# Silu gates by one hyperbolic tangent read from PSUM, and reciprocal roots by a power on POOL, in the last two layers of a four-layer kernel

## The chip, the cores and the metric

The kernel runs on one core of a Trainium2 chip. The metric is device time in microseconds (us) of one execution; lower is better. The engines are called as in the profile: PE (TensorE, matrix products; PEld is its loading of weights), DVE (VectorE), ACT (ScalarE), POOL (GpSimd) and SP (SyncE, which only starts transfers here).

## The reference

Four layers run over 512 tokens of width 1024 in float32. The first two (attention over selected keys with a short convolution, then attention with a compressed latent, each with a feed-forward part) are not touched. The last two, with 256 context tokens beside the 512, are called layer 2 and layer 3 here, as in the kernel. Both project to q, k, v and z of width 2048, normalize q and k by head, attend, and gate the result with silu(z) ahead of an output product:

```python
def project(u, n):                      # layers 2 and 3
    q, k, v, z = jnp.split(u @ w_in, 4, axis=-1)
    q = rms_norm(q.reshape(bsz, n, HEADS, 64), qn_g)
    k = rms_norm(k.reshape(bsz, n, HEADS, 64), kn_g)
...
# layer 2: differential attention, 16 pairs of heads, values of width 128
w = p[:, :, 0] - lam * p[:, :, 1]
o = rms_norm(o, subln_g) * (1.0 - lam_init)
return (o.reshape(bsz, n, D_INNER) * jax.nn.silu(z)) @ w_out
# layer 3: neighbourhood attention, 32 heads, a band of keys and the context
out_l = (o_l * jax.nn.silu(z_l)) @ w_out
```

with `rms_norm(x, g) = x * rsqrt(mean(x*x) + EPS) * g` and `silu(z) = z * sigmoid(z)`.

## The kernel before, in words

**Products.** Every float32 product is made of three matmuls: both operands are split into a high part in fp32r and a rest. `mm3` (L587 to L589) issues high by high, low by high and high by low. The weights are split on chip: ACT casts the high part (`w_hi`, L276), POOL subtracts it (`w_lo`, L280). So each 256 columns of q, k, v or z are 24 matmuls of 256 columns on PE.

**Staging.** `second(L, nx)` runs layer L of the last two. It projects the q and k pieces of the first of 8 groups of heads, with nothing else to do beside them, and then runs a loop, `diff_run` (layer 2, 12 steps per group) or `na_run` (layer 3, 16 steps per group). A step takes one unit of 128 queries through a pipeline written out by hand: `A` scores on PE (`s`, L2105 and L2106 in layer 2, L2277 and L2278 in layer 3), `B` the row minimum of the negated scores on DVE, `E` the exponential on ACT, `Dm` the division by the row sums on DVE (L2138 to L2140, L2296 and L2297), `T` transposes on PE (L2152, L2304) whose result ACT and DVE copy out of PSUM, and `G` the product with the values. In layer 2, `Hn` and `H2` then normalize 6 blocks by head and multiply by the gate (L2193, L2194).

**What fills the steps.** The dictionaries `fill`, `extra` and `early` hold, by step number, what else is issued there: `fill` the projection pieces of the next group's q, k and v and of this group's z, `extra` and `early` small things. A matmul piece is one of the 24-matmul blocks, and its second function takes the result out of PSUM. `defer` puts a function off to the next step. Each engine takes its instructions in the order in which they are issued here, so an instruction that waits holds everything behind it on its engine.

**Gates.** A z piece (`z_piece`, 256 columns, 80 of them) is copied by ACT from PSUM to `SZ`. `gates_at` later takes `SZ` in chunks of 128 columns: ACT makes exp(-z) into `ge`, a step later DVE adds 1 (L1829) and takes the reciprocal (L1830), and POOL multiplies `SZ` by it (L1831). In layer 2 there are 12 chunks per group, in layer 3 8; the last of layer 3 falls into step 1 of the next group.

**Reciprocal roots.** `finish` makes those of q and k when all their sums of squares (`ssq`, `ssk`, 16 or 24 per partition) are there: DVE prepares, ACT takes Ln and Exp, DVE does one step of Newton's method (`rstd_parts`, L422 to L434), and then POOL multiplies the raw k or q tiles (`st`, L1800). In layer 2, q's roots are not multiplied in but go into `B` as a scale. `stack` transposes the result (L1843), ACT and DVE write it as `KH`, `KL`, `QS` (high and low parts), and `dup` has POOL issue two transfers that copy `KH` and `KL` to the other 64 partitions (L1867), for which `A` of the next group waits.

**PSUM.** During the loops the buffers called `mm`, which take projection pieces and `G`, are 2 in layer 2 and 3 in layer 3.

Of the kernel before, what the change touches and what calls it, by code (L numbers as in the profile page):

```python
# [12 lines left out]
F32 = mybir.dt.float32  # L13
# [12 lines left out]
EPS = 1e-6  # L26
NEG = -1e30
TAKEN = -3e38
UNIT = 1104
LNEXP = "natural_log_exp_and_others"  # L30


# [348 lines left out]
class Net:  # L381
# [54 lines left out]
    def rstd(s, r, ss, inv_n):  # L436
        for _ in s.rstd_parts(r, ss, inv_n):
            pass

    def run(s):  # L440
        nc, tc, io = s.nc, s.tc, s.io
        with ExitStack() as top:
# [22 lines left out]
            s.zero = s.const.tile([128, 1], F32, name="zero")  # L465
            nc.vector.memset(s.zero, 0.0)
            s.dram = s.pool("dram", 1, space=DRAM)
            s.xd = [s.dram.tile([4, 128, D], F32, name=f"xs{l}") for l in range(3)]
# [1167 lines left out]
    def tables2(s, pool, tmp):  # L1636
# [11 lines left out]
        def compute():  # L1648
# [20 lines left out]
            gs = pool.tile([128, 1], F32, name="gs")  # L1669
            nc.vector.tensor_scalar(gs, s.p("subln"), 1.0 - lam_init, None, OP.mult)  # L1670
            t2["nlam"], t2["gs"] = nlam, gs
# [3 lines left out]
    def second(s, L, nx):  # L1675
# [108 lines left out]
        def finish(n, g, k):  # L1784
            r = g2.tile([128, 24], F32, name=f"r{n}")
            rs = s.rstd_parts(r[:, :k], SS[n][:, :k], 1.0 / 64)
            next(rs)

            def two():
                next(rs, None)  # L1790
                if n == "q":
                    nc.vector.tensor_scalar(r[:, :k], r[:, :k], 0.125, None, OP.mult)
                    if diff:
                        r2 = g2.tile([128, 24], F32, name="nrq")
                        nc.vector.tensor_scalar(r2, r, -1.0, None, OP.mult)
                        scal[g] = r, r2
                        return
                for i in range(k // 4):
                    x = rawt[n][:, i].rearrange("p (h d) -> p h d", d=64)
                    nc.gpsimd.tensor_tensor(x, x, r[:, 4 * i:4 * i + 4].unsqueeze(2).to_broadcast([128, 4, 64]), OP.mult)  # L1800

            s.defer(two)

        def z_piece(g, b, t0):
            box = {}

            def mm():
                if t0 == 0:
                    hold("z", [f"z{L}:{g}:{b}"])
                box["ps"] = ps = s.mm.tile([128, 512], F32, name="mm")[:, :256]  # L1810
                for h in range(2):
                    s.fmm(ps, U["z"], uh, ul, t0, 256, ks=range(4 * h, 4 * h + 4))
                    yield

            return mm, lambda: s.act(SZ[g][b][:, t0:t0 + 256], box["ps"], AF.Copy)

        def gates_at(ts, g, chunks):

            e = {}

            def one(b, c):
                z = SZ[g][b][:, c * 128:(c + 1) * 128]
                e[b, c] = g2.tile([128, 128], F32, name="ge", bufs=3 if diff else 4)
                s.act(e[b, c], z, AF.Exp, scale=-1.0)

            def two(b, c):
                z = SZ[g][b][:, c * 128:(c + 1) * 128]
                x = e[b, c]
                nc.vector.tensor_scalar(x, x, 1.0, None, OP.add)  # L1829
                nc.vector.reciprocal(x, x)  # L1830
                nc.gpsimd.tensor_tensor(z, z, x, OP.mult)  # L1831

            for t, bc in sorted([(t + 1, (0, bc)) for t, bc in zip(ts, chunks)] + [(t, (1, bc)) for t, bc in zip(ts, chunks)]):
                put((early, extra)[bc[0]], t, lambda bc=bc: (two, one)[bc[0]](*bc[1]))

# [67 lines left out]
        for g in range(8):  # L1903
# [3 lines left out]
            if diff and g < 7:  # L1907
# [4 lines left out]
                for j in range(6):  # L1912
                    put(fill, t0 + j, *qk[2 * j:2 * j + 2])
                at = (6, 6, 7, 8, 8, 9, 9, 10, 11, 12, 13, 14) if g < 6 else (6, 7, 7, 8, 8, 9, 13, 13, 14, 14, 15, 15)
                gates_at([t0 + t for t in at], g, [(b, c) for b in range(2) for c in range(6)])
                for t, f in zip((6, 7, 8, 9), stacks("q", 0) + stacks("k", 0)):
# [5 lines left out]
            elif diff:  # L1922
                for t, x in zip(Z7, zz):
                    put(fill, t0 + t, x)
                put(extra, t0 + 2, lambda: y_tile(), *[lambda b=b: y_dma(b) for b in range(5)])
                gates_at([t0 + t for t in (4, 5, 6, 7, 8, 9, 10, 11, 12, 13, 14, 15)], g, [(b, c) for b in range(2) for c in range(6)])
                put(extra, t0 + 5, lambda: y_dma(5))
                for b in range(8):
                    put(early, t0 + Y7[b], lambda b=b: y_split(b))
            else:  # L1930
                if g < 7:
                    vv = [piece("v", g + 1, i) for i in range(6)]
                    for t, x in zip((0, 1, 2, 3, 4, 5, 6, 7, 8, 9, 10, 11, 12, 13) + ((13, 14, 14, 15, 15, 16) if g < 6 else (14, 15, 15, 16, 16, 17)), qk + zz + vv):
                        put(fill, t0 + t, x)
                    gates_at([t0 + t for t in (12, 13, 13, 14, 14, 15, 15, 16)], g, [(b, c) for b in range(2) for c in range(4)])
                    for t, f in zip((12, 13, 14), stacks("q", 0) + stacks("k", 0)):
# [6 lines left out]
                else:  # L1943
                    for t, x in zip(Z73, zz):
                        put(fill, t0 + t, x)
                    gates_at([t0 + t for t in (7, 8, 9, 10, 11, 12, 13, 14)], g, [(b, c) for b in range(2) for c in range(4)])
                    put(extra, t0 + 2, *[lambda b=b: y_dma(b) for b in range(6)])
                    for b in range(8):
                        put(extra, t0 + Y73[b], lambda b=b: y_split(b))
            if g == 7:  # L1950
                for j, (c, i) in enumerate([(c, i) for c in range(nq) for i in range(nq)][:12 if diff else 10]):
                    acc[c, i] = st[:, j]
                    put(fill, t0 + (O7 if diff else O73)[j], o_piece(c, i))

        order = [("q", i) for i in START[L][0]] + [("k", i) for i in START[L][1]] + [(n, i) for n in "qk" for i in START[L][2] if i < nq or n == "k"]
        after = {order.index(("q", 3)): [lambda: s.W.release(s.W.i - 2)]} if diff else {}
# [28 lines left out]
        run(c)  # L1985
        s.drain()
        ictx.close()
        if diff:
# [88 lines left out]
    def diff_run(s, c):  # L2077
# [30 lines left out]
        def B(u):  # L2108
            g, p, t = u
            x = d[u]  # L2110
            nrq = c.scal[g][1]
            for j in range(2):
                h = 4 * t + 2 * p + j
                S = x["s"][j]
                nb = s.sml.tile([128, 1], F32, name="df_nb")
                nc.vector.tensor_tensor_reduce(S, S, s.zero.to_broadcast(list(S.shape)), nrq[:, h:h + 1], 3e38, OP.add, OP.min, nb)
                x["nb"].append(nb)
# [53 lines left out]
        def Hn(g, p):  # L2171
            o, ss, oe = O[g, p]
            v, y, a = [s.sml.tile([128, 6], F32, name=f"df_{k}") for k in "vya"]
            nc.vector.scalar_tensor_tensor(oe, oe, EPS, oe, OP.mult, OP.mult)
            nc.vector.scalar_tensor_tensor(v, ss, 1.0 / 128, oe, OP.mult, OP.add)
            s.act(y, v, AF.Ln)
            s.act(y, y, AF.Exp, scale=-0.5)

            def two():
                nc.vector.tensor_tensor(a, y, y, OP.mult)  # L2180
                nc.vector.tensor_tensor(a, a, v, OP.mult)
                nc.vector.tensor_scalar(a, a, -0.5, 1.5, OP.mult, OP.add)
                nc.vector.tensor_tensor(y, y, a, OP.mult)
                nc.gpsimd.tensor_tensor(o, o, y.unsqueeze(2).to_broadcast([128, 6, 128]), OP.mult)

            s.defer(two)
# [45 lines left out]
    def na_run(s, c):  # L2232
# [60 lines left out]
        def Dm(u):  # L2293
            x = d[u]
            r = s.sml.tile([128, 1], F32, name="na_r")
            nc.vector.reciprocal(r, x["sm"])  # L2296
            nc.vector.tensor_scalar(x["P"], x["P"], r, None, OP.mult)  # L2297

# [92 lines left out]
```

## Time and profile before

| | |
|---|---|
| median of 3 runs | 3179.25 us (3178.51 to 3179.38) |
| profiled execution | 3187.93 us |
| its span, first to last instruction | 3186.2 us |
| PE busy | 3063.2 us (96%) |
| POOL, DVE, ACT busy | 1742.4, 1908.9, 1613.7 us (55%, 60%, 51%) |
| granted TensorE clock, mean | 0.988 of full speed |

The three runs were taken without the profiler; the profiled execution is another one, 8.7 us longer than their median. The views of the trace refer to its span, in microseconds from its start. Layer 2 runs from about 1405 to 2410 (its loop 1458 to 2290), layer 3 from 2410 to the end (its loop 2454 to 3120). A busy share of 96% says that PE has little to wait for anywhere; where it waits, and for whom, is read by stretches.

### The profile page before, as it was taken

The page shows a single profiled execution, that of the slowest core. Times are in us where ns is not written, and L with a number is a line of the kernel's source. Part 1 is how long each engine was busy: PE and PEld are TensorE (multiplying, and loading weights), DVE is VectorE, ACT ScalarE, POOL GpSimd, SP SyncE. Part 2 cuts the span into 40 slices and gives each one's busy share as a digit, 9 for nine tenths or more (in the row PEclk, how much of TensorE's full clock was granted, in tenths as well). Part 3 has the DMA queues.
Part 4 walks back from the last instruction along what each step waited for, and adds up shares of the span by engine and source line. Part 5 has one row for each costly group of instructions (what it writes and reads, how often), then busy time and mean ns, then how long its engine had stood idle before and what let it go on. Part 6 is the DMA issues. An engine that isn't in the chain of part 4 may idle for free.

```text
span 3186.2 us, 59888 instructions
## 1 busy us (share of the span) xinstructions
PE 3063.2 (96%) x22868; PEld 2883.9 (91%) x22868; DVE 1908.9 (60%) x4161; ACT 1613.7 (51%) x3811; POOL 1742.4 (55%) x2398
## 2 busy tenths in 40 slices
PE   8999999998999999998999999998999999999989
PEld 7898889887999988898999999998999999999989
DVE  4875423345774333455777777777445777777764
ACT  4544533345775433344655555555325656555652
POOL 5543466664563666666556655563356455555545
PEclk9999999999999999999999999999999999999989
DMA  3122333434233444422222222213333233333234
GB/s 123 60 74 82 104 126 132 147 115 142 92 95 109 137 142 136 133 94 76 69 70 61 75 69 66 67 61 102 116 105 87 74 88 84 90 90 89 86 96 140
DMA packets 104555, 310.89 MB, mean 98 GB/s; under 512 B 19902, under 2 KB 33470, under 8 KB 100684
## 3 DMA queue, kind: packets, MB, share of 16 engines
q1 hardware_dynamic: 94908, 271.60, 26.4%
q0 software_dynamic: 7776, 31.46, 4.3%
q10 hardware_dynamic: 1584, 4.00, 0.4%
q8 instruction: 181, 2.97, 0.4%
q14 instruction: 106, 0.87, 0.1%
HBM read 258.73 MB, written 23.12 MB: 88 GB/s over the span
## 4 chain that ended last, share of the span: by engine, by line
PE 62%; DVE 4%; ACT 3%; DMA 3%; POOL 2%; issue 1%; SPq 0%; DVEq 0%; ACTq 0%; POOLq 0%
PE mm L587 16%; PE mm L589 15%; PE mm L588 15%; PE mm L2165 3%; DMA KL<-KL 2%; PE s L2105 2%; PE tp L2304 2%; PE tp L2152 1%; PE s L2106 1%; POOL w_lo L280 1%; PE mm L2319 1%; PE mm L2314 1%; ACT X L413 1%; PE s L2278 1%; PE tp L1843 1%
## 5 line engine op out<-in xcount | busy, mean ns | idle before, releaser
L280 POOL TENSOR_TENSOR w_lo<-w_raw,w_hi 128x256 fp32r<-128x256 f32 (+2 forms) x1446 | 1145.7, 825 | 816.2 <-ACT w_hi L276 786.3
L587 PE MATMUL mm<-w_hi,hh 128*128 128x256 f32 (+2 forms) x2752 | 803.0, 292 | 11.6 <-ACT w_hi L276 4.4
L588 PE MATMUL mm<-w_lo,hh 128*128 128x256 f32 (+2 forms) x2752 | 784.7, 285 | 5.4 <-POOL w_lo L280 3.9
L589 PE MATMUL mm<-w_hi,hl 128*128 128x256 f32 (+2 forms) x2752 | 783.8, 285 | 1.1 <-POOL hl L416 1.1
L587 PEld LDWEIGHTS mm<-w_hi,hh 128*128 128x128 f32 x2752 | 525.8, 191 | 22.1 <-ACT df_sq L413 8.5
L588 PEld LDWEIGHTS mm<-w_lo,hh 128*128 128x128 f32 x2752 | 526.5, 191 | 14.2 <-POOL w_lo L280 8.9
L589 PEld LDWEIGHTS mm<-w_hi,hl 128*128 128x128 f32 x2752 | 525.0, 191 | 2.5 <-POOL hl L416 1.8
L276 ACT CAST w_hi<-w_raw 128x1024 fp32r<-128x1024 f32 (+2 forms) x371 | 383.0, 1036 | 210.5 <-PE mm L589 171.1
L587 PE MATMUL mm<-hh,w_hi 128*128 128x256 f32 (+1 forms) x1408 | 455.5, 324 | 3.0 <-DVE M L1092 2.9
L588 PE MATMUL mm<-hl,w_hi 128*128 128x256 f32 (+1 forms) x1408 | 449.0, 319 | 0.6
L589 PE MATMUL mm<-hh,w_lo 128*128 128x256 f32 (+1 forms) x1408 | 447.6, 318 | 0.6 <-DVE w_lo L280 0.6
L587 PEld LDWEIGHTS mm<-hh,w_hi 128*128 128x128 f32 x1408 | 266.8, 190 | 30.8 <-issue 5.2
L587 PE MATMUL mm<-w_hi,gh 128*128 128x256 f32 x1024 | 287.8, 281 | 0.0
L589 PE MATMUL mm<-w_hi,gl 128*128 128x256 f32 x1024 | 287.1, 280 | 0.1
L588 PEld LDWEIGHTS mm<-hl,w_hi 128*128 128x128 f32 x1408 | 266.9, 190 | 22.3 <-DVE hl L347 1.7
L588 PE MATMUL mm<-w_lo,gh 128*128 128x256 f32 x1024 | 287.0, 280 | 0.0
L589 PEld LDWEIGHTS mm<-hh,w_lo 128*128 128x128 f32 x1408 | 266.5, 189 | 21.4 <-DVE w_lo L280 1.0
L416 DVE TENSOR_TENSOR gl<-rsq,gh 128x512 fp32r<-128x512 f32 x64 | 46.2, 721 | 268.7 <-ACT gh L413 268.7
L587 PEld LDWEIGHTS mm<-w_hi,gh 128*128 128x128 f32 x1024 | 193.2, 189 | 0.4
L589 PEld LDWEIGHTS mm<-w_hi,gl 128*128 128x128 f32 x1024 | 193.0, 188 | 0.5 <-DVE gl L416 0.5
L588 PEld LDWEIGHTS mm<-w_lo,gh 128*128 128x128 f32 x1024 | 193.0, 188 | 0.3
L1831 POOL TENSOR_TENSOR SZ<-SZ,ge 128x128 f32<-128x128 f32 x154 | 80.3, 523 | 162.2 <-DVE ge L1829 68.9
(385 smaller groups left out, 6948.8 us busy)
## 6 DMA issues: line engine op xcount, KB each, us to landing
w_raw<-in_w SPq DMA_DIRECT2D x352, 512.0 KB, 3.6
modw<-in_mod SPq DMA_DIRECT2D x24, 1024.0 KB, 5.7
KH<-KH POOLq DMA_DIRECT2D x32, 384.0 KB, 3.5
KL<-KL POOLq DMA_DIRECT2D x32, 384.0 KB, 4.9
xs<-X SPq DMA_DIRECT2D x12, 512.0 KB, 3.6
X<-xs SPq DMA_DIRECT2D x12, 512.0 KB, 8.4
yd<-ob SPq DMA_DIRECT2D x16, 384.0 KB, 2.5
w_raw<-in_w SPq DMA_DIRECT2D x8, 552.0 KB, 3.6
```

What stands on the lines that cost most here:

```text
L276: nc.scalar.copy(hi[:, :m], raw[:, :m])
L280: (eng or nc.gpsimd).tensor_tensor(lo[:, c], raw[:, c], hi.bitcast(F32)[:, c], OP.subtract)
L413: return s.nc.scalar.activation(out, in_, func, bias=bias, scale=scale, **kw)
L416: (eng or s.nc.vector).tensor_tensor(lo, x, hi.bitcast(F32), OP.subtract)
L587: mm(ps, ah, bh, start=first, stop=False)
L588: mm(ps, ah, bl, start=False, stop=False)
L589: mm(ps, al, bh, start=False, stop=last)
L1831: nc.gpsimd.tensor_tensor(z, z, x, OP.mult)
L1843: nc.tensor.transpose(pt[:, j], rawt[n][:, i, pr * 128:(pr + 1) * 128], s.ident)
L2105: nc.tensor.matmul(o, q, KH[:, h, a:b], start=True, stop=False)
L2165: nc.tensor.matmul(ps, x["w"][:, k], V[g][:, kb, p * 128:(p + 1) * 128], start=k == 0, stop=k == nk - 1)
L2304: nc.tensor.transpose(t[:, k], x["P"][:, k * 128:(k + 1) * 128], s.ident)
```

## The change

1. **Gates.** The evacuation of a z piece becomes ACT's Tanh of z/2, read from PSUM, and one DVE instruction that reads PSUM again and writes (tanh(z/2) + 1) * z, which is twice silu(z). `gates_at` and all its chunks are gone. The factor of two is taken out elsewhere: by `gs` in layer 2, by a second scalar in the instruction that divides the probabilities in layer 3. In layer 2 the DVE instruction is issued at once, in layer 3 a step later.
2. **Roots.** In `finish` and in `Hn`, POOL raises to the power -0.5 (a new `rstd_pool`). DVE's and ACT's parts are gone. It is still followed by the same multiplications on POOL.
3. **Tables.** ACT holds the functions that it can compute in tables. Three loads of a table are added: Tanh's ahead of each of the two layers' first q piece, and that of logarithms behind layer 2's loop.

```diff
+    def rstd_pool(s, r, ss, inv_n, c, eps=EPS):
+
+        s.nc.gpsimd.tensor_scalar(r, ss, inv_n, eps, OP.mult, OP.add)
+        s.nc.gpsimd.tensor_tensor(r, r, s.mhalf.to_broadcast(list(r.shape)), OP.pow)
+        if c != 1.0:
+            s.nc.gpsimd.tensor_scalar(r, r, c, None, OP.mult)
...
-            nc.vector.tensor_scalar(gs, s.p("subln"), 1.0 - lam_init, None, OP.mult)
+            nc.vector.tensor_scalar(gs, s.p("subln"), 0.5 * (1.0 - lam_init), None, OP.mult)
...
         def finish(n, g, k):
-            r = g2.tile([128, 24], F32, name=f"r{n}")
-            rs = s.rstd_parts(r[:, :k], SS[n][:, :k], 1.0 / 64)
-            next(rs)
+            r = g2.tile([128, 24], F32, name=f"r{n}")[:, :k]
             def two():
-                next(rs, None)
-                if n == "q":
-                    nc.vector.tensor_scalar(r[:, :k], r[:, :k], 0.125, None, OP.mult)
-                    if diff:
-                        r2 = g2.tile([128, 24], F32, name="nrq")
-                        nc.vector.tensor_scalar(r2, r, -1.0, None, OP.mult)
-                        scal[g] = r, r2
-                        return
+                s.rstd_pool(r, SS[n][:, :k], 1.0 / 64, 1.0 if n == "k" else -0.125 if diff else 0.125)
+                if n == "q" and diff:
+                    scal[g] = r
+                    return
...
-            return mm, lambda: s.act(SZ[g][b][:, t0:t0 + 256], box["ps"], AF.Copy)
-        def gates_at(ts, g, chunks):
...
+            def ev():
+                ps, e = box["ps"], g2.tile([128, 256], F32, name="ge")
+                s.act(e, ps, AF.Tanh, scale=0.5)
+                mult = lambda: nc.vector.scalar_tensor_tensor(SZ[g][b][:, t0:t0 + 256], e, 1.0, ps, OP.add, OP.mult)
+                mult() if diff else s.defer(mult)
+            return mm, ev
...
+        nc.scalar.preload_act_table_set(TANHEXP)
         order = [("q", i) for i in START[L][0]] + [("k", i) for i in START[L][1]] + [(n, i) for n in "qk" for i in START[L][2] if i < nq or n == "k"]
...
         run = s.diff_run if diff else s.na_run
         run(c)
         s.drain()
+        if diff:
+            nc.scalar.preload_act_table_set(LNEXP)
...
         def Hn(g, p):
             o, ss, oe = O[g, p]
-            v, y, a = [s.sml.tile([128, 6], F32, name=f"df_{k}") for k in "vya"]
-            nc.vector.scalar_tensor_tensor(oe, oe, EPS, oe, OP.mult, OP.mult)
-            nc.vector.scalar_tensor_tensor(v, ss, 1.0 / 128, oe, OP.mult, OP.add)
-            s.act(y, v, AF.Ln)
-            s.act(y, y, AF.Exp, scale=-0.5)
+            y = s.sml.tile([128, 6], F32, name="df_y")
             def two():
-                nc.vector.tensor_tensor(a, y, y, OP.mult)
-                nc.vector.tensor_tensor(a, a, v, OP.mult)
-                nc.vector.tensor_scalar(a, a, -0.5, 1.5, OP.mult, OP.add)
-                nc.vector.tensor_tensor(y, y, a, OP.mult)
+                nc.gpsimd.tensor_tensor(oe, oe, oe, OP.mult)
+                nc.gpsimd.tensor_scalar(oe, oe, 128 * EPS, None, OP.mult)
+                nc.gpsimd.tensor_tensor(ss, ss, oe, OP.add)
+                s.rstd_pool(y, ss, 1.0 / 128, 1.0, 0.0)
                 nc.gpsimd.tensor_tensor(o, o, y.unsqueeze(2).to_broadcast([128, 6, 128]), OP.mult)
...
-            nc.vector.tensor_scalar(x["P"], x["P"], r, None, OP.mult)
+            nc.vector.tensor_scalar(x["P"], x["P"], r, 0.5, OP.mult, OP.mult)
```

PE's and SP's instructions and their order are the same in both kernels. Three places show the others.

On POOL, at the end of layer 2's start, ahead of the first transfers of `KH` and `KL`, there stood before (`X_66` to `X_69` are scratch, `ctk` and `snk` tables of the rotation):

```order
L1773 TENSOR_TENSOR st<-X_66,X_67 128x256
L1766 TENSOR_TENSOR X_68<-st,ctk 128x256
L1771 TENSOR_TENSOR X_69<-st,snk 128x8x16 x2
L1773 TENSOR_TENSOR st<-X_68,X_69 128x256
L1800 TENSOR_TENSOR st<-st,rk 128x256 x6
L280 TENSOR_TENSOR w_lo<-w_raw,w_hi 128x256 x8
L1867 DMA KH<-KH 64x1536
```

and now there stands:

```order
L1783 TENSOR_TENSOR st<-X_66,X_67 128x256
L443 TENSOR_SCALAR rq<-ssq 128x24
L444 TENSOR_TENSOR rq<-rq,mhalf 128x24
L446 TENSOR_SCALAR rq<-rq 128x24
L1776 TENSOR_TENSOR X_68<-st,ctk 128x256
L1781 TENSOR_TENSOR X_69<-st,snk 128x8x16 x2
L1783 TENSOR_TENSOR st<-X_68,X_69 128x256
L443 TENSOR_SCALAR rk<-ssk 128x24
L444 TENSOR_TENSOR rk<-rk,mhalf 128x24
L1804 TENSOR_TENSOR st<-st,rk 128x256 x6
L281 TENSOR_TENSOR w_lo<-w_raw,w_hi 128x256 x8
L1859 DMA KH<-KH 64x1536
```

Five instructions of 24 elements a partition, two of them powers, have come in front of the six multiplications by `rk` and of the transfers. Nothing has left POOL there.

On ACT, at the beginning of layer 2's start, the difference is the load of the table between the normalization of the last tokens and the first evacuations of q (`st`, `sq`):

```order
 L414 ACTIVATE rs_y<-nf_ss,eps 128x2
 L414 ACTIVATE rs_y<-rs_y 128x2
 L414 ACTIVATE nf_y<-X_69,nf_r 128x512
+L1942 ACT_TABLE_LOAD
 L414 ACTIVATE st<-mm 128x256
 L414 ACTIVATE sq<-mm 128x256
```

The load is in front of the evacuations, and nothing else moved there.

On DVE, in layer 3, from the end of step 0 to `Dm` of step 2 of a group, there stood before (`ptl` is the low part that `T` leaves, `na_r` the reciprocal row sum of `Dm`, and the two rows called ISA are `B`):

```order
L416 TENSOR_TENSOR ptl<-tp,pth 128x512
L1829 TENSOR_SCALAR ge<-ge 128x128
L1830 RECIPROCAL ge<-ge 128x128
L2296 RECIPROCAL na_r<-na_s 128x1
L2297 TENSOR_SCALAR X_67<-X_67,na_r 128x512
L2326 TENSOR_TENSOR X_69<-mm,X_68 64x448
L2326 TENSOR_TENSOR X_69<-mm,X_68 64x64
L1777 TENSOR_REDUCE ssq<-X_69 128x4
L1856 SCALAR_TENSOR_TENSOR KL<-tp,par,KH 64x256 x2
L2286 ISA s_32737,na_nb<-s_32737,bm_29271 128x512
```

and now there stands:

```order
L417 TENSOR_TENSOR ptl<-tp,pth 128x512
L2282 RECIPROCAL na_r<-na_s 128x1
L2283 TENSOR_SCALAR X_67<-X_67,na_r 128x512
L2312 TENSOR_TENSOR X_69<-mm,X_68 64x448
L2312 TENSOR_TENSOR X_69<-mm,X_68 64x64
L1787 TENSOR_REDUCE ssq<-X_69 128x4
L1848 SCALAR_TENSOR_TENSOR KL<-tp,par,KH 64x256 x2
L2272 ISA s_31998,na_nb<-s_31998,bm_28670 128x512
```

One chunk of a gate is gone from in front of `Dm`, and with it everything behind it stands two instructions earlier; the DVE instructions that replace the gates stand behind the z pieces, in steps 11 to 14.

## Rows read from the trace of the kernel before

**Rows 1.** Stretches: us; busy PE, PEld, DVE, ACT, POOL; clock; DMA share, GB/s.

```profile
1460.00:2140.00 680.00, 666.89 (x5380) 644.75 (x5380) 495.49 (x1108) 383.68 (x1143) 404.33 (x615) 1.00 0.22 66
...
2460.00:3020.00 560.00, 552.74 (x4409) 537.02 (x4408) 416.26 (x948) 335.48 (x808) 287.35 (x428) 1.00 0.30 85
```

**Rows 2.** Waits of PE, 2460:3020 (layer 3's loop): total us, times, longest.

```profile
PE tp L2304 <- DVE X L2297: 4.7, 11, 0.5
PE s L2278 <- DMA KL<-KL: 2.3, 6, 1.0
```

**Rows 3.** Waits of PE, 1460:2140 (layer 2's loop).

```profile
PE s L2105 <- ACT X L413: 5.8, 8, 0.7
PE tp L1843 <- DVE ob L2194: 3.8, 6, 0.6
```

**Rows 4.** Timeline of DVE in layer 3, steps 1 and 2: start, us, [idle before <-releaser].

```profile
2713.13 0.22 DVE L1829 TENSOR_SCALAR ge<-ge 128x128 f32<-128x128 f32 x1
2713.38 0.95 DVE L1830 RECIPROCAL ge<-ge 128x128 f32<-128x128 f32 x1
...
2717.34 0.70 DVE L2286 CUSTOM_DVE_ANT_0 s<-s,bm 128x512 f32<-128x512 f32 x1
```

**Rows 5.** Timeline of PE in the same step 2.

```profile
2718.89 0.28 PE L588 MATMUL mm<-w_lo,hh 128*128 128x256 f32 x1
2719.01 0.28 PE L589 MATMUL mm<-w_hi,hl 128*128 128x256 f32 x1
2719.78 0.63 PE L2304 MATMUL tp<-ident,X 128*128 128x128 f32 x4 [0.49 <-DVE X L2297]
```

**Rows 6.** Timeline of ACT, just before `KH` of layer 3's next group.

```profile
2692.62 0.51 ACT L413 ACTIVATE ge<-SZ 128x128 f32<-128x128 f32 x2
```

**Rows 7.** Timeline of POOL, then of PE, where layer 3's last group begins.

```profile
3020.02 2.98 POOL L280 TENSOR_TENSOR w_lo<-w_raw,w_hi 128x256 fp32r<-128x256 f32 x4 [1.17 <-ACT w_hi L276]
3022.97 0.88 POOL L1831 TENSOR_TENSOR SZ<-SZ,ge 128x128 f32<-128x128 f32 x2
3023.79 0.57 POOL L1867 DMA_DIRECT2D KH<-KH  x1
...
3021.86 0.63 PE L2304 MATMUL tp<-ident,X 128*128 128x128 f32 x4 [2.03 <-DVE X L2297]
3029.42 0.35 PE L2277 MATMUL s<-KH,QS 128*128 128x256 f32 x1 [2.25 <-DMA KH<-KH]
```

**Rows 8.** Timeline in layer 2's loop: ACT in a steady group, PE in the last.

```profile
1830.84 0.38 ACT L413 ACTIVATE SZ<-mm 128x256 f32<-128x256 f32 x1
...
2246.54 0.39 PE L2105 MATMUL s<-KH,QS 128*128 128x256 f32 x1 [1.30 <-ACT X L413]
```

**Rows 9.** Timeline of POOL, then of PE, at the end of layer 2's start.

```profile
1442.22 3.48 POOL L1800 TENSOR_TENSOR st<-st,rk 128x256 f32<-128x256 f32 x6
...
1451.16 0.59 POOL L1867 DMA_DIRECT2D KH<-KH  x1
...
1457.81 0.77 PE L2105 MATMUL s<-KH,QS 128*128 128x512 f32 x1 [8.22 <-DMA KH<-KH]
```

**Rows 10.** Timeline of ACT (a table load), then of PE at the beginning of layer 2's start.

```profile
56.05 1.28 ACT L569 ACT_TABLE_LOAD   x1
...
1408.61 0.39 PE L587 MATMUL mm<-w_hi,hh 128*128 128x256 f32 x1 [1.81 <-ACT sq L413]
```

**Rows 11.** Groups by line and shape: costs of small instructions (busy, mean ns).

```profile
L858 POOL TENSOR_SCALAR wi<-tk 128x16 f32<-128x16 f32 x4 | 1.5, 371 | 0.3
L821 POOL TENSOR_TENSOR kr<-rk_a,rk_b 128x32 f32<-128x32 f32 x4 | 1.0, 256 | 0.3
L347 DVE SCALAR_TENSOR_TENSOR hl<-tp,par,hh 128x256 fp32r<-128x256 f32 x64 | 29.5, 481 | 34.0 <-ACT hh L413 33.8
```

**Rows 12.** Timeline of POOL: multiplications by `rk`, layer 2's loop, layer 3's start.

```profile
1828.53 3.48 POOL L1800 TENSOR_TENSOR st<-st,rk 128x256 f32<-128x256 f32 x6
...
2437.44 3.48 POOL L1800 TENSOR_TENSOR st<-st,rk 128x256 f32<-128x256 f32 x6 [5.76 <-DVE rk L434]
```

More of the change, by code (lines that the diff above doesn't have):

```diff
@@ L30 @@
 LNEXP = "natural_log_exp_and_others"
+TANHEXP = "exp_and_others"
 def plan():
@@ L466, in run @@
             nc.vector.memset(s.zero, 0.0)
+            s.mhalf = s.const.tile([128, 1], F32, name="mhalf")
+            nc.vector.memset(s.mhalf, -0.5)
             s.dram = s.pool("dram", 1, space=DRAM)
@@ L1813, in mm @@
                     yield
-            return mm, lambda: s.act(SZ[g][b][:, t0:t0 + 256], box["ps"], AF.Copy)
-        def gates_at(ts, g, chunks):
[L1819 to L1834, printed above, removed]
+            def ev():
[4 more added lines that the diff above has]
+            return mm, ev
         def stack(n, pr, tiles):
@@ L1913, in second @@
                     put(fill, t0 + j, *qk[2 * j:2 * j + 2])
-                at = (6, 6, 7, 8, 8, 9, 9, 10, 11, 12, 13, 14) if g < 6 else (6, 7, 7, 8, 8, 9, 13, 13, 14, 14, 15, 15)
-                gates_at([t0 + t for t in at], g, [(b, c) for b in range(2) for c in range(6)])
                 for t, f in zip((6, 7, 8, 9), stacks("q", 0) + stacks("k", 0)):
@@ L1925, in second @@
                 put(extra, t0 + 2, lambda: y_tile(), *[lambda b=b: y_dma(b) for b in range(5)])
-                gates_at([t0 + t for t in (4, 5, 6, 7, 8, 9, 10, 11, 12, 13, 14, 15)], g, [(b, c) for b in range(2) for c in range(6)])
                 put(extra, t0 + 5, lambda: y_dma(5))
@@ L1934, in second @@
                         put(fill, t0 + t, x)
-                    gates_at([t0 + t for t in (12, 13, 13, 14, 14, 15, 15, 16)], g, [(b, c) for b in range(2) for c in range(4)])
                     for t, f in zip((12, 13, 14), stacks("q", 0) + stacks("k", 0)):
@@ L1945, in second @@
                         put(fill, t0 + t, x)
-                    gates_at([t0 + t for t in (7, 8, 9, 10, 11, 12, 13, 14)], g, [(b, c) for b in range(2) for c in range(4)])
                     put(extra, t0 + 2, *[lambda b=b: y_dma(b) for b in range(6)])
@@ L2110, in B @@
             x = d[u]
-            nrq = c.scal[g][1]
+            nrq = c.scal[g]
             for j in range(2):
```

## The prediction

> **What bounds the kernel now.** I read the page first: PE is busy 96% of the span, so a change to the other engines is worth only what PE waits for in the two layers it touches. Then the stretches [rows 1]: in layer 3's loop PE is busy 552.74 of 560 us, so at most 7.3 us are to be had in those groups; in layer 2's loop it is 666.89 of 680, 13.1 us. DVE is the most loaded of the helpers (495 of 680 and 416 of 560), POOL is idle 276 of 680 and 273 of 560. DVE's load bounds nothing by itself; the question is which waits of PE end at work that goes away. So I went on to PE's waits by releaser.
>
> In layer 3's loop there are two kinds [rows 2]. `T` waits 11 times, 4.7 us in all, for the division in `Dm`; and `A` waits 6 times, 2.3 us, for the copy of `KL`. The timeline of DVE in one group shows where the first comes from [rows 4]: the last chunk of a gate (0.22 us for the addition, 0.95 for the reciprocal) stands in step 1 in front of `Dm`, and `B` of step 2 starts as late as 2717.34; PE then waits at 2719.78 [rows 5]. The second kind goes back to ACT: two exponentials of gates, 0.51 us, run at 2692.62, straight ahead of the `KH` that the transfers wait for [rows 6].
>
> In layer 2's loop the waits are others [rows 3]: 5.8 us for ACT's exponential in `E`, since PE reuses its scores' buffer, and 3.8 us where `H2`'s DVE result holds a transpose buffer. For the first, the steady group shows ACT doing the evacuation of a z piece (0.38 us at 1830.84) in front of that exponential [rows 8].
>
> **The change part by part.** The gates' old chunks go: 160 times 0.22 + 0.95 us on DVE [rows 4] is 187 us. The new instruction is a scalar-tensor-tensor of 128x256 out of PSUM; its nearest row takes 0.481 us on average [rows 11], so 80 of them are 38 us. DVE gains about 150 us, and all of it matters only at the waits above.
>
> *Layer 3, `T` waits for `Dm`.* With the chunk gone DVE is 1.17 us earlier in steps 1 and 2, more than the longest wait of 0.5. What a wait costs is more than its listed length: PE's starts are 0.12 us apart at speed (2718.89, 2719.01) and 0.77 across the wait, so 0.65 are lost where 0.49 are listed [rows 5]. 4.7 times 0.65/0.49 is 6.2 us. Bounds: 3, if ACT's exponential, which is next in the chain, is then late itself, to 6.2. I take **-6.2**, since DVE, and not ACT, is late in that row.
>
> *Layer 3, `A` waits for `KL`.* 0.51 us of exponentials leave ACT ahead of `KH` in each of the groups, and the 6 waits together are 2.3 [rows 2, 6]. 0 to 2.3; I take **-2.0**.
>
> *Layer 3, into the last group.* `T` waits 2.03 us for `Dm` at 3021.86, and `A` 2.25 for `KH` at 3029.42 [rows 7]. If only the first went, the second would grow by as much. But the transfer moves too: POOL issues it at 3023.79 behind two multiplications of gates (0.88 us, gone) and behind `w_lo`, which waited 1.17 for a cast that stands on ACT behind an exponential, that behind `B`, and that behind a chunk of 1.17. 0.88 + 1.17 = 2.05, so the transfer keeps pace: **-2.0** (0 to -2.0), and the 2.25 stay.
>
> *Layer 2's loop.* Tanh takes the place of the copy ahead of the exponential, in the same order, so the 5.8 stay; the 3.8 don't hang on gates. In the last group one wait of 1.30 us at 2246.54 [rows 8] stands behind `Hn`'s DVE instructions and its Ln and Exp on ACT, which go to POOL: **-1.3** (0 to -1.3). The powers of the steady groups, two of q and k and two of `Hn` for each group of 12 steps, are covered by POOL's idle 41% [rows 1]; the multiplications by `rk` start there at 1828.53 after other work, not after DVE [rows 12]. If that cover went, every group would pay, which is part of a rival.
>
> *Layer 2's start.* Here the change costs. No gates exist yet, and PE's first scores wait 8.22 us for `KH`, which POOL issues at 1451.16 behind the multiplications by `rk` at 1442.22 [rows 9]. The five new instructions on POOL stand in front of these and of the transfers. Three are plain ones with scalars; the nearest row takes 0.371 us [rows 11], so 1.1. Two are powers of 128x24, call one X. No row has one. From below: a plain 128x32 on POOL takes 0.256 [rows 11], so 0.24 for 24. From above: as long as the six multiplications of 128x256 by `rk`, 3.48 us [rows 9], which is 64 plain elements' work for each element. Between, the one non-linear function of this kernel that has a plain neighbour of its size is DVE's reciprocal, 0.95 against 0.22, 4.3 times [rows 4]; 4.3 times 0.24 is X = 1.05, which I take. 2X + 1.1 = 3.2 us, all on the path. Ahead of that, the table load, 1.28 us [rows 10], comes on ACT right before the first evacuation, for which PE waits 1.81 already at 1408.61, so it is paid in full: 1.3. Together **+4.5** (2.9 with X of 0.24, 9.4 with 3.48).
>
> The Trainium skill ("ScalarE: Activation LUTs", What ACT_TABLE_LOAD costs) puts a switch to a different set at about 2.66 us, the load and a drain behind it of nearly the same length; the load agrees with this trace's row of 1.28, a drain is not shown in it. By that, the start would pay 1.4 us more, an estimate from that page, and the sum would be 5.3 instead of 6.7 us.
>
> *Layer 3's start.* POOL sat idle 5.76 us until DVE had `rk` [rows 12], so one power instead of five instructions on two engines costs nothing up to several times X. The table load again stands ahead of the first evacuations; with 4 buffers of PSUM there PE can run on: **+0.3** (0 to 1.3). The load behind layer 2's loop lies on an ACT that has nothing left to do.
>
> **Sum.** -6.2 - 2.0 - 2.0 - 1.3 + 4.5 + 0.3 = -6.7. The profiled execution took 3187.93 us, so 3181.2; the median of the runs is 8.7 below its own profile, so **3172.5 us**. A measurement of this kernel can tell about 0.2%, 6.4 us, from no change; the forecast stands on that edge.
>
> **The rivals.**
> 1. *A z piece's PSUM buffer is held longer, and PE waits for it in layer 2* (the other sign). There are 2 `mm` buffers. The copy freed one in 0.38 us [rows 8]; now Tanh and then a DVE instruction of 0.48, queued behind `B` and a copy, must be done. 48 pieces run there. At 0.5 us for half of them it is +12, so 3184.5; from a mean of 0.27 us per piece (13.1/48) the kernel is slower by over 0.2%. For it: DVE is busy 73% there. Against it: the two chunks that each piece had on DVE, 2.3 us, are gone from the same steps, and the larger waits of PE name no evacuation of z now [rows 3].
> 2. *The power is dear.* Place: layer 2's start, twice X. With X = 3.48 it is 4.9 us more, 3177.4; from X = 7.6 it is slower by over 0.2%, and then the steady groups' multiplications by `rk` would be late too.
> 3. *The waits of layer 3 are replaced.* Without the chunk, `T` waits for ACT's exponential or for PE's own scores. Half of 6.2 and none of the `KL` waits: 5.1 less gained, 3177.6.
> 4. *More is gained.* DVE's relief also halves layer 2's two waits (4.8 of 9.6 us): 3167.7.
>
> **How the numbers follow.** The forecast, within some 4 us, gets 0.45, of which I put 0.28 beyond the 0.2% and 0.17 within. Rival 4 gets 0.15 (faster), rival 3 0.15 (within), rival 1 0.15 (0.05 within, 0.10 slower), rival 2 0.10 (0.03 within, 0.07 slower). Faster 0.43, the same 0.40, slower 0.17. The range goes from 3164, somewhat below rival 4, to 3184, near rival 1's case, and leaves out about 2 in 10.
>
> **What would show it.** Right: in the changed trace `T`'s waits for `Dm` are gone from layer 3's groups, `KL`'s are near nothing, and PE's first scores in layer 2 wait some 3 us longer for `KH`. Wrong: a power on POOL far from 1.05 us; waits of PE for a buffer named by the new DVE instruction on `SZ`; layer 3's `T` still waiting, then for another releaser.

## The result: slower by 1.5%

The changed kernel took 3228.61 us (median of 5 runs, 3222.70 to 3233.54), the kernel before 3179.38 us beside it (5 runs). The ratio is 1.0148, with a 95% interval from 1.0133 to 1.0163: about 48 us slower, where 7 us faster was forecast, and outside the range. The profiled execution of the changed kernel took 3233.54 us, its span is 3231.1.

Where the time went is read by cutting both spans at the same events of PE: the first score matmul of layer 2's loop, the last one, and the same in layer 3 (their starts in PE's timelines; differences are worked out from them). Beginnings of layer 2's loop scatter by some 5 us between kernels that do the same up to there, so smaller differences in the first column mean nothing. Nor do 4 us in layer 3's loop: the kernel before with one queue moved (below), equally fast, has 650.5 us there.

| us | up to layer 2's loop | layer 2's loop | between | layer 3's loop | behind it |
|---|---|---|---|---|---|
| before | 1457.8 | 797.4 | 198.8 | 654.8 | 77.3 |
| changed | 1471.0 | 790.5 | 209.1 | 684.3 | 76.1 |
| difference | +13.2 | -6.8 | +10.3 | +29.5 | -1.2 |

So layer 2's loop became shorter, and what was lost was lost in the two starts and, above all, in layer 3's loop. The waits of PE, first in layer 2's start (1400:1500), then in layer 3's loop without its first and last group (2480:3060): what waits and its releaser, total us, times, longest.

```profile
PE s L2095 <- DMA KH<-KH: 7.9, 1, 7.9
PE tp L1835 <- POOL st L1804: 7.4, 1, 7.4
PE mm L597 <- ACT sq L414: 3.3, 1, 3.3
...
PE s L2263 <- DMA KH<-KH: 14.8, 6, 3.4
PE s L2264 <- DMA KL<-KL: 7.8, 6, 1.7
PE tp L2290 <- DVE X L2283: 2.1, 6, 0.6
```

Against [rows 2] the waits for `Dm` fell from 11 to 6, those for `KL` grew from 2.3 to 7.8 us, and 14.8 us of waits for `KH` are new. In the start, 7.4 us in which transposes wait for POOL's `st` stand ahead of the wait for `KH`, which had been 8.22 alone [rows 9]. The stretch of layer 3's groups had a clock of 1.00 [rows 1]; now (stretches, columns as there, 2475:3060):

```profile
2475.00:3060.00 585.00, 560.31 (x4381) 545.05 (x4380) 348.17 (x811) 320.09 (x727) 311.58 (x410) 0.97 0.29 79
```

0.97, not 1.00: after each of the new waits PE runs a few microseconds at its lower level of 1.2 GHz before it is back at 2.4. In PE's timeline 13 to 21 matmuls of 256 columns behind the wait start 0.21 us apart and not 0.12, which costs another 1.2 to 1.9 us in each group.

What the power costs is in the groups by line and shape (busy us, mean ns):

```profile
L444 POOL TENSOR_TENSOR rk<-rk,mhalf 128x24 f32<-128x24 f32 x16 | 67.7, 4232 | 1.3
L444 POOL TENSOR_TENSOR rq<-rq,mhalf 128x16 f32<-128x16 f32 x8 | 23.4, 2924 | 0.7
L444 POOL TENSOR_TENSOR df_y<-df_y,mhalf 128x6 f32<-128x6 f32 x16 | 21.7, 1355 | 1.3
L443 POOL TENSOR_SCALAR rk<-ssk 128x24 f32<-128x24 f32 x16 | 3.4, 213 | 7.6 <-DVE ssk L1787 6.4
```

4.2 us for 24 elements a partition, 2.9 for 16, 1.36 for 6: a line through them is 0.41 us and 0.157 us for each element. A plain instruction with scalars on the same 24 elements, in the last row, takes 0.21. The power is 20 times that; I had taken 1.05 us.

What that does in a group of layer 3 is seen on POOL (timeline; start, us, and in brackets the idle time before and its releaser):

```profile
2698.10 0.21 POOL L443 TENSOR_SCALAR rk<-ssk 128x24 f32<-128x24 f32 x1
2698.40 4.29 POOL L444 TENSOR_TENSOR rk<-rk,mhalf 128x24 f32<-128x24 f32 x1
2702.77 3.47 POOL L1804 TENSOR_TENSOR st<-st,rk 128x256 f32<-128x256 f32 x6
2706.20 5.81 POOL L281 TENSOR_TENSOR w_lo<-w_raw,w_hi 128x256 fp32r<-128x256 f32 x8
2716.01 0.79 POOL L2245 TENSOR_TENSOR bm<-na,X 128x256 f32<-128x256 f32 x1 [4.00 <-DMA X<-in_rpb]
2716.74 0.29 POOL L1850 CAST QS<-QS 128x128 fp32r<-128x128 f32 x1
2717.00 2.83 POOL L281 TENSOR_TENSOR w_lo<-w_raw,w_hi 128x256 fp32r<-128x256 f32 x4
2719.79 0.64 POOL L1859 DMA_DIRECT2D KH<-KH  x1
```

and, for the same moments, on SP, which issues the loads of weights (`w_raw`) and of the bias (`X` and `bm` from `in_rpb`) in order:

```profile
2698.04 14.32 SPq L264 DMA_DIRECT2D w_raw<-in_w  x3
2712.46 0.39 SPq L2242 DMA_DIRECT2D X<-in_rpb  x1
2712.90 1.11 SPq L2244 DMA_DIRECT2D bm<-in_rpb  x2
2719.86 0.33 SPq L264 DMA_DIRECT2D w_raw<-in_w  x1
```

SP holds three weight loads for 14.32 us, because the buffers that they fill come free only when POOL has made the `w_lo` behind the power; the same SP row takes 9.72 us in the kernel before. The bias load behind them goes out at 2712.46, POOL sits idle 4.00 us for it with `bm`, and the last `w_lo` of the group is pushed to 2717.00. In the kernel before POOL waits there as well, and nearly as long:

```profile
2685.97 0.74 POOL L2259 TENSOR_TENSOR bm<-na,X 128x256 f32<-128x256 f32 x1 [3.87 <-DMA X<-in_rpb]
```

So the idle time did not shrink by the power's 4.3 us, it only came later. POOL's idle time was no cover: it was spent waiting for a load that itself waited for POOL. In the kernel before, the last `w_lo` ended 4.2 us before ACT had written `KH`; now it ends 1.0 us after that. It sets off one more weight load at 2719.86, 0.07 us behind the copy of `KH` at 2719.79. In the kernel before that load went out at 2689.80 and the copy at 2694.27. What the collision costs is in the lists of DMA issues (KB each, us from issue to landing), here of the group behind the one shown, in the changed kernel (2803:2820) and then in the kernel before (2775:2790):

```profile
KH<-KH POOLq DMA_DIRECT2D x1, 384.0 KB, 7.0
KL<-KL POOLq DMA_DIRECT2D x1, 384.0 KB, 8.1
```

```profile
KH<-KH POOLq DMA_DIRECT2D x1, 384.0 KB, 3.5
KL<-KL POOLq DMA_DIRECT2D x1, 384.0 KB, 4.5
```

In the six groups of layer 3 from the second to the seventh, the first copies of a group, which PE waits for, take 6.2 to 7.3 us (`KH`) and 7.4 to 8.4 (`KL`); in the kernel before, 3.5 in five of them and 5.1 in one, and 4.4 to 5.3. The medians of a whole run, which the experiments below are compared by, are 6.4 and 7.5 against 3.5 and 4.9; half of the 32 copies behind them are layer 2's, whose medians are 3.6 and 4.9 in the changed kernel, and 3.5 and 4.8 before.

### The profile page after: what moved, and what is told of

It reads as the page before. It is cut to its first block, busy times and chain, and to the rows that moved or that the text cites. A ratio compares the mean times of both kernels' runs of the same rounds, so it can differ in the third digit from the quotient of the medians.

```text
span 3231.1 us, 59188 instructions
## 1 busy us (share of the span) xinstructions
PE 3072.8 (95%) x22868; PEld 2897.4 (90%) x22868; DVE 1677.3 (52%) x3674; ACT 1564.8 (48%) x3558; POOL 1831.8 (57%) x2398
## 4 chain that ended last, share of the span: by engine, by line
PE 57%; POOL 6%; ACT 4%; DMA 4%; DVE 3%; issue 1%; SPq 0%; POOLq 0%; ACTq 0%; DVEq 0%
PE mm L597 14%; PE mm L599 14%; PE mm L598 14%; POOL w_lo L281 3%; PE mm L2155 3%; DMA KL<-KL 2%; PE s L2095 2%; PE s L2096 1%; PE tp L2142 1%; PE tp L2290 1%; ACT X L414 1%; POOL rk L444 1%; PE s L2264 1%; PE mm L2305 1%; PE mm L2300 1%
## 5 line engine op out<-in xcount | busy, mean ns | idle before, releaser
L597 PEld LDWEIGHTS mm<-w_hi,hh 128*128 128x128 f32 x2752 | 535.0, 194 | 23.8 <-ACT df_sq L414 8.5
L598 PEld LDWEIGHTS mm<-w_lo,hh 128*128 128x128 f32 x2752 | 535.1, 194 | 15.6 <-POOL w_lo L281 10.0
L599 PEld LDWEIGHTS mm<-w_hi,hl 128*128 128x128 f32 x2752 | 533.6, 194 | 5.3 <-POOL hl L417 4.7
L597 PEld LDWEIGHTS mm<-hh,w_hi 128*128 128x128 f32 x1408 | 266.9, 190 | 29.5 <-issue 5.2
L414 ACT ACTIVATE wt<-tp 128x512 f32<-128x512 f32 (+1 forms) x96 | 50.6, 527 | 267.7 <-PE tp L2142 267.7
```

The lines of the kernel that those rows point to most:

```text
L414: return s.nc.scalar.activation(out, in_, func, bias=bias, scale=scale, **kw)
L597: mm(ps, ah, bh, start=first, stop=False)
L598: mm(ps, ah, bl, start=False, stop=False)
L599: mm(ps, al, bh, start=False, stop=last)
```

## The experiments

Theory P: the power is the loss, in the starts by its own time on POOL, in layer 3 through the queues as just read (this second half is theory C). Rival Q: the gates are the loss, by the buffer that the new DVE instruction holds. The kernel before was run beside each set of experiments (medians 3183.05, 3183.29 and 3182.63 us), and the ratios are to it. In the recorded expectations e5 is the experiment headed "The queue in layer 3" and e6 the one headed "Other gates"; e1 below is the first one, and e9 the last.

**The power's price taken away** (the roots are not computed):

```diff
-        s.nc.gpsimd.tensor_tensor(r, r, s.mhalf.to_broadcast(list(r.shape)), OP.pow)
+        s.nc.gpsimd.tensor_tensor(r, r, s.mhalf.to_broadcast(list(r.shape)), OP.mult)
```

> The changed kernel with POOL's power replaced by a product on the same tiles, so that the roots are not computed; order and number of instructions stay. Theory P (the power's 4.2 us on POOL is the loss, in layer 2's start twice and in every group of layer 3): about 57 us less than the changed kernel, 3165 to 3174, groups of layer 3 below 82.7 us. Rival Q (the PSUM buffer held by DVE, or something else of the gates, is the loss): 3210 or more.

3167.48 us (3166.62 to 3172.43), 0.9954 of before (0.9937 to 0.9971). Q falls: the gates' and the tables' instructions are all there. The product takes 0.27 us, a sixteenth of the power, and `KH` lands as before:

```profile
L444 POOL TENSOR_TENSOR rk<-rk,mhalf 128x24 f32<-128x24 f32 x16 | 4.3, 271 | 1.3
...
KH<-KH POOLq DMA_DIRECT2D x32, 384.0 KB, 3.6
```

By stretches it is +2.1 up to layer 2's loop, -7.1, -1.5, -13.0, -1.2 against before: with a cheap root the change would have been a gain, and of about twice the size of my sum (15.6 us by the medians; the traced execution of before was a long one).

**The roots alone**: the kernel before with the new `finish`, `Hn` and `rstd_pool`, and with the gates and tables of before:

```diff
-            rs = s.rstd_parts(r[:, :k], SS[n][:, :k], 1.0 / 64)
...
+                s.rstd_pool(r, SS[n][:, :k], 1.0 / 64, 1.0 if n == "k" else -0.125 if diff else 0.125)
```

> The kernel before with only the roots moved to POOL's power; gates and tables as before. P: no gain at the gates, all of the loss: 3225 to 3240. Q: within 10 us of before.

3218.50 us, 1.0110 of before (1.0095 to 1.0125): 35 us, most of the loss but less than expected. The waits in layer 3's loop (2460:3050) are of another mixture:

```profile
PE s L2277 <- DMA KL<-KL: 9.4, 7, 1.5
PE tp L2303 <- DVE X L2296: 7.0, 13, 2.0
PE s L2276 <- POOL SZ L1834: 6.5, 5, 1.6
PE s L2276 <- DMA KH<-KH: 5.8, 2, 3.5
```

Here POOL still had gates to multiply ahead of the copies, which spread them and the weight load apart: that load goes out 1.9 us ahead of the copy, and `KH` lands in 3.8 us in the median. So layer 3's loop, 677.3 us, lost 22.5 us without the collision. The way was another: POOL's multiplications of the gates came late, and with them the release of the buffers `ge`, for which ACT waited with the exponential of a gate that stands ahead of `KH`. ACT's timeline in a group:

```profile
2710.39 0.31 ACT L413 ACTIVATE ge<-SZ 128x128 f32<-128x128 f32 x1 [2.13 <-POOL SZ L1834]
```

It is so ahead of `KH` in all of the seven groups behind the first, 2.1 to 2.9 us each; in the kernel before none of these exponentials waits. So the two halves of the change don't add up: with the gates in place the power delays `KH` through `ge`, and with the gates gone POOL issued the copies at the very moment of the load. In layer 2 the groups are 101.6 us apart, like the changed kernel's 101.7 and unlike the 102.1 of before: what layer 2's loop gained is from the roots that left DVE and ACT, and not from the gates.

**The gates alone**: the changed kernel with `finish` and `Hn` of before.

```diff
-                s.rstd_pool(r, SS[n][:, :k], 1.0 / 64, 1.0 if n == "k" else -0.125 if diff else 0.125)
+            rs = s.rstd_parts(r[:, :k], SS[n][:, :k], 1.0 / 64)
```

> The changed kernel with the roots as before, by Ln and Exp. Ln and Tanh are in different tables, so some 100 loads stand on ACT, two or four at each root. P: no wait for KH of over 1 us in layer 3, but waits of PE for ACT behind pairs of loads of 2.6 us: 3180 to 3240. Q: waits of PE for a buffer that the DVE product holds, as in the changed kernel.

3208.09 us in a single run, against 3183.05 of before. Ln is in another table than Tanh, and the loads are these (group by line):

```profile
L414 ACT ACT_TABLE_LOAD x98 | 125.7, 1283 | 1.7
```

In layer 2's loop PE waits for ACT and for what ACT delays (1460:2290):

```profile
PE s L2101 <- ACT X L414: 12.1, 13, 2.6
PE tp L2148 <- DVE KL L417: 11.0, 7, 1.9
PE mm L2161 <- ACT sq L414: 10.3, 6, 1.7
```

The loop takes 823.6 us, 26 more than before, while layer 3's takes 650.5, which is within the scatter named above. No wait names the DVE product on a buffer. In layer 3 there is one wait for `KH` of over 1 us, 4.2 at the last group, against the expectation. So this form of gate needs a root that isn't made by Ln, and the two halves of the change hang together for that reason.

**The queue in layer 3**: the changed kernel with the bias loads on another queue.

```diff
-            nc.sync.dma_start(rpb, io["rpb"][h, :, 0:256])
+            nc.scalar.dma_start(rpb, io["rpb"][h, :, 0:256])
...
-                nc.sync.dma_start(t[a:a + 64, 0, 128 - 2 * a:256 - 2 * a], io["rpb"][h, a:a + 64, 256:384])
+                nc.scalar.dma_start(t[a:a + 64, 0, 128 - 2 * a:256 - 2 * a], io["rpb"][h, a:a + 64, 256:384])
```

> The changed kernel with layer 3's small loads of the bias (in_rpb) issued from ACT's queue and not from SP's, where they stand behind weight loads that wait for POOL. Theory C (in layer 3 the power's delay goes through SP's queue into bm, from there into the last w_lo of a group, and so sets off a weight load at the very moment of the KH and KL transfers, which then take twice as long): KH lands in under 4.5 us, not 6.4, groups of layer 3 take 83 to 85 us, not 87 to 88, in all 15 to 30 us less than the changed kernel, 3200 to 3214. Rival D (KH is late because it is issued late, behind the power): 3222 or more.

3185.98 us, 1.0009 of before (1.0000 to 1.0018): 43 us less than the changed kernel, more than expected, with the power at its full price. POOL in a group of layer 3:

```profile
2680.06 4.30 POOL L444 TENSOR_TENSOR rk<-rk,mhalf 128x24 f32<-128x24 f32 x1
2684.44 3.48 POOL L1804 TENSOR_TENSOR st<-st,rk 128x256 f32<-128x256 f32 x6
2687.87 5.81 POOL L281 TENSOR_TENSOR w_lo<-w_raw,w_hi 128x256 fp32r<-128x256 f32 x8
2693.64 0.74 POOL L2245 TENSOR_TENSOR bm<-na,X 128x256 f32<-128x256 f32 x1
2694.32 0.29 POOL L1850 CAST QS<-QS 128x128 fp32r<-128x128 f32 x1
2694.58 2.84 POOL L281 TENSOR_TENSOR w_lo<-w_raw,w_hi 128x256 fp32r<-128x256 f32 x4
2700.78 0.64 POOL L1859 DMA_DIRECT2D KH<-KH  x1 [3.36 <-ACT KH L414]
```

`bm` no longer waits, POOL is done 3.36 us before `KH` is, and the copies land in 3.6 and 5.0 us (medians). Groups of layer 3 between the first and the last are 81.3 to 82.5 us apart, where they were 86.1 to 88.4 in the changed kernel and about 82.7 before; the loop takes 643.5 us, 41 less than the changed kernel's.

**The same move without the power**: the kernel before with the edit of the last experiment.

> The kernel before with the loads of the bias issued from ACT's queue, as in e5. If their place matters only where the power has delayed POOL (theory C): within 4 us of before. If moving them is worth as much by itself: 3140 to 3160.

3182.63 us, 0.9999 of before (0.9990 to 1.0008). The place of those loads is worth nothing until something delays POOL; so what the last experiment won back is the power's own damage. Of theory C, the way of the delay through SP's queue stands by these two runs; that the collision, and not the lateness of the copies, made the waits for `KH` is read from the changed trace further below.

**The power in pieces**, from the second group on:

```diff
                 nc.vector.tensor_reduce(ss[:, 4 * i:4 * i + 4], sq.rearrange("p (h d) -> p h d", d=64), AX.X, OP.add)
+                if g:
+                    s.rstd_pool(ss[:, 4 * i:4 * i + 4], ss[:, 4 * i:4 * i + 4], 1.0 / 64, 1.0 if n == "k" else -0.125 if diff else 0.125)
```

> The changed kernel with the power, from the second group on, taken in pieces of 4 columns as soon as a projection piece's sums are there, not of 16 or 24 at the end. POOL's total grows by some 2.5 us per group (a power costs 0.41 us and 0.158 for each column), but only about 1 us stands ahead of the multiplications by rk. P and C: layer 3's groups back to 82 to 84 us, 3190 to 3205; layer 2's start as in the changed kernel. If POOL's total load were the loss: 3228 or more.

3197.29 us, 1.0041 of before (1.0027 to 1.0055), 31 us less than the changed kernel though POOL's powers take longer in sum. Layer 3's loop takes 643.5 us, as with the bias moved; the starts keep their losses. Two groups of layer 2 are 5 us longer than the others there, behind waits for `Dm` on DVE (5.9 us in two waits). In each of them one instruction of `Dm` lasted six times its median of 1.02 us:

```profile
1741.08 6.01 DVE L2132 SCALAR_TENSOR_TENSOR X<-X,df_rb,X 128x768 f32<-128x768 f32 x1
```

It ends 0.8 us behind an unbroken run of POOL's instructions of 128x256 (1734.51 to 1746.27), as does the other one (2050.87, 6.02 us). That POOL held it is not shown; no run tests it. What a power would take on DVE instead of POOL no run shows either.

**Other gates**: no power and no other table.

```diff
+            def three(x, e):
+                s.act(e, x, AF.Exp, scale=-1.0)
+                s.act(e, e, AF.Ln, bias=s.tiny, scale=2.0 ** -20)
+                s.act(e, e, AF.Exp, bias=s.lift, scale=-1.0)
```

(`tiny` is 2 to the -20 and `lift` -20 ln 2, which keep Ln's argument small.)

> No power and no other table: the roots as before, the gate as exp(-ln(1 + exp(-z))) by three ACT instructions of 256 columns in the table that is loaded anyway; in layer 2 on a copy of z a step later with POOL's product, in layer 3 from PSUM with DVE's product. DVE loses its reciprocals, POOL keeps its old work. If the gain of the change is DVE's chunks and its loss the power and the tables: 3165 to 3173, faster than before. Rival (ACT's two further passes delay the exponentials of E): 3180 or more.

3171.05 us, 0.9961 of before (0.9948 to 0.9975): the gain of layer 3 without the roots. Its groups between the first and the last are 81.1 to 82.2 us apart, those of layer 2 102.0, as before. With the bias loads moved too:

> The kernel of e6 with the bias loads by ACT. No power delays POOL there, so within 4 us of e6.

3173.94 us, 0.9969 (0.9958 to 0.9980), the same.

**The power kept out of the starts**: the bias loads by ACT, and

```diff
-        nc.scalar.preload_act_table_set(TANHEXP)
...
+            rs = iter(()) if g else s.rstd_parts(r, SS[n][:, :k], 1.0 / 64)
...
+                if g:
+                    s.rstd_pool(r, SS[n][:, :k], 1.0 / 64, c)
...
+        nc.scalar.preload_act_table_set(TANHEXP)
         run = s.diff_run if diff else s.na_run
```

> The kernel of e5 (bias loads by ACT) with the first group's roots by Ln, Exp and Newton's step as before and Tanh's table loaded only when the loop begins, so that neither a power nor a table load stands in the two starts. Theory: e5 less the two starts' losses, some 10 us in layer 2's and 8 in layer 3's, 3164 to 3170, faster than before. If the powers in the loops still cost: 3175 or more.

3165.64 us (3159.93 to 3169.69), 0.9944 of before (0.9931 to 0.9956), the fastest here. By stretches 1456.8, 790.4, 198.7, 641.8, 76.1 us: both starts are those of the kernel before, both loops are as short as with a free power. Its waits in layer 2's start (1400:1470) are back to one long one:

```profile
PE s L2103 <- DMA KH<-KH: 8.7, 1, 8.7
PE s L2104 <- DMA KL<-KL: 1.2, 1, 1.2
PE mm L597 <- ACT sq L414: 0.9, 1, 0.9
```

So the powers in both loops, two of q and k for each group and in layer 2 two of `Hn`, cost nothing once the queue is in order.

## Why the prediction was wrong

**The step that failed first is the price of the power, X.** I took 1.05 us, from what DVE's reciprocal costs against a plain instruction, and 3.48 as the upper end; it is 4.2. DVE's ratio of 4.3 between a function and a plain instruction did not carry over: on POOL it is 16 to 20. With 4.2 in the sum, layer 2's start would have cost 2 times 3.15, 6.3 us, more than +4.5; that alone gives 3179, no change. So the size of X explains only a part of the 48 us.

**The step that failed worse is the cover.** Of layer 3's loop I worked out what the removed gates would give back, and no cost of the powers at all; of layer 3's start I wrote that POOL's 5.76 us of idle time would hide several times X. Both took idle time for slack. In the start the idle time ended when `rk` was ready, so whatever makes `rk` later makes all behind it later. From the end of the last sum of squares to the multiplications by `rk` the five old instructions had needed only 1.3 us (2436.10 to 2437.44 [rows 12]); the power's way takes 4.65 (2449.15 to 2453.80). The row of DVE before, then two of POOL now:

```profile
2435.68 0.42 DVE L1777 TENSOR_REDUCE ssk<-X 128x4 f32<-128x256 f32 x1 [2.42 <-ACT X L413]
```

```profile
2449.24 0.22 POOL L443 TENSOR_SCALAR rk<-ssk 128x24 f32<-128x24 f32 x1 [6.38 <-DVE ssk L1787]
...
2453.80 3.47 POOL L1804 TENSOR_TENSOR st<-st,rk 128x256 f32<-128x256 f32 x6
```

The stretch between the loops grew by 10.3 us. e9, which has no power there, has it back, and so has e1 (197.3 us), where the table load still stands: it was the power, with q's 2.9 us ahead of this one, and not the load. In the loop, POOL waited for SP, and SP for POOL, so the power's 4.3 us went around that ring, and then pushed a weight load onto the copies that PE waits for: the 29.5 us. The move of the bias loads showed it, since POOL's work is the same in both kernels. In the sum this is a term that is missing: the power in layer 3's loop and start stood there at nothing. Rival 2 had the right culprit; its price, and the point from which it would make the kernel slower, X of 7.6, were worked out from layer 2's start alone, and so too mild.

**Layer 2's start** was the right place, with sizes off: the stretch up to the loop grew by 13.2 us in this trace, by 9.2 and 10.5 in those of e5 and of the power in pieces, which do the same up to there. The added wait was not one for `KH`, as the sign to look for had it (7.9 us after 8.22), but 7.4 us of the transposes ahead of it. The plain instructions with scalars were 0.21 to 0.28 us, not 0.37; the powers 8.4 us together, not 2.1; the wait behind the table load rose from 1.81 to 3.3, by 1.5 us for a load of 1.28. The Trainium skill ("ScalarE: Activation LUTs", What ACT_TABLE_LOAD costs) adds a drain of about 1.38 us to a load of about 1.28. The load agrees with this trace; the drain does not show in it: the first evacuation follows at once on ACT in this timeline of the changed kernel.

```profile
1408.39 1.28 ACT L1942 ACT_TABLE_LOAD   x1
1409.68 0.38 ACT L414 ACTIVATE st<-mm 128x256 f32<-128x256 f32 x1
```

**Layer 2's steady groups.** That POOL's idle time covers the powers there was right (101.7 us a group, not 102.1). That Tanh's place leaves the 5.8 us for ACT as they are was right too: 5.8 in the changed kernel. That nothing but 1.3 us would be gained was too little: 6.8 were, of which each of the steady groups gives 0.4, from the roots.

**Rival 1** did not happen. The DVE product took 0.42 us, against the 0.48 that I took, and no wait names it on a buffer.

**Layer 3's gains** came, and about as large as the -10.2: with the power's price away (e1) the loop is 13.0 us shorter than in the trace of before and 8.6 shorter than with the equally fast kernel before with the bias loads moved. Of the two waits of `T` for `Dm` in each group one is gone, and the other, 0.5 us before, is still 0.3 to 0.6 (2.1 us in all, where the forecast had none). The prediction's own -6.2 and -2.0 go past the 7.3 us that it gives as the most to be had in those groups; the second to the seventh take 488.4 us in e1, and 496.4 and 496.2 in those two traces, about 8 more, so PE's idle time was no hard bound.

**The collision or the lateness.** Of the changed kernel's extra 29.5 us, the trace tells which of the two made the waits for `KH`. In the six groups with waits of 1.5 to 3.4 us the copy went out 1.0 to 2.0 us after ACT had written `KH` (0.3 in the kernel before), landed 6.2 to 7.3 us after that, and PE came to need it 5.9 us after ACT had written it. With the 3.5 us that a landing mostly took before, it would have been there 4.5 to 5.5 us after ACT, in time; with a landing of 7.0 and the issue of before, PE would have waited 1.4 us. So (an estimate from these rows) lateness alone would have cost no wait for `KH` there, and the longer landing is the larger part; only at the last group, 5.4 us late, it is lateness above all, with a wait of 8.0 us.

That the weight load is what lengthens the landing rests on its company and not on a run of its own. The load goes out 0.07 to 0.09 us behind the copy in all of the changed kernel's seven groups behind the first. It goes out 3.9 to 4.5 us ahead in six of before (landings of 3.5 us, once 5.1), and 1.9 us ahead in six of the kernel with the roots alone (3.6 to 3.7, once 4.8). In e1, with no power to delay anything, it is 0.09 us behind at the last group, and `KH` takes 7.0 us there. How the 29.5 us divide among waits, clock and lateness as a whole stays open.

## What to carry to other kernels

An engine's idle time covers a new instruction only if what ended it comes no later for that instruction; follow the releaser back, through the queue of SP too, and see whether the way leads to the engine itself. A function that has no row on an engine should be measured by itself before it is put on a chain, or tried with a plain instruction in its place, which here told that everything else in the change was a gain. And a load that a buffer's release sets off moves with the engine that releases it: look at what it will then collide with.

## What the runs showed of the hardware

A power of two float32 tensors on POOL takes 0.41 us and 0.157 us for each element of a partition (1.36, 2.92 and 4.2 us for 6, 16 and 24); at 24 elements that is 16 times a product of the same tiles (0.27 us) and 20 times a plain instruction with scalars (0.21). A copy of 384 KB from POOL's queue took 6.2 to 7.3 us in groups where a load of 512 KB went out within 0.1 us of it, and 3.5 (once 5.1) in the kernel before, where that load went out some 4 us ahead. A load of ACT's table took 1.28 us in the mean of 98, and in the two starts of the changed kernel the next instruction on ACT began 0.01 to 0.02 us behind it.
